# A fused decoder block on one core: another model of time for ordering each engine's instructions

## The chip, the cores and the metric

The kernel runs on one core of a Trainium2 chip. A core has five engines that run beside each other, each with its own queue of instructions that it takes in order: TensorE (matrix products, PE in the profile), VectorE (DVE), ScalarE (ACT), GpSimd (POOL) and SyncE (SP, which here only issues DMA transfers). They wait for each other by semaphores. The metric is the device time of the whole program in microseconds, and lower is better.

## The reference

One layer of a decoder block on x of 1024 rows and 1024 columns. A normalised input goes through one wide projection, whose columns feed two attention branches and their gates.

```python
h = rms_norm(x, norm_in[layer])
proj = h @ w_in[layer]
(dq, dk, dv, dgate, cq, ckv, kr, mgate, g_diff, g_mla) = jnp.split(proj, split_idx, axis=-1)
# differential branch: 4 heads, 2 score maps of 64 columns each, values of 128
dq, dk = apply_rope(dq, cos_d, sin_d), apply_rope(dk, cos_d, sin_d)
o_diff = causal_multimap_attention(dq, dk, dv, [1, -lam], 64 ** -0.5)
o_diff = rms_norm(o_diff, diff_subln[layer]) * (1.0 - lambda_init) * silu(dgate)
# latent branch: 4 heads, queries from rank 384, keys and values from rank 256, 64 rotary columns
q = rms_norm(cq, mla_q_norm) @ w_uq
kv = rms_norm(ckv, mla_kv_norm) @ w_ukv
o_mla = causal_multimap_attention([q_nope, rope(q_rope)], [k_nope, rope(kr)], v, [1], 192 ** -0.5)
o_mla = o_mla * silu(mgate)
merged = sigmoid(g_diff) * (o_diff @ w_proj_diff) + sigmoid(g_mla) * (o_mla @ w_proj_mla)
return rms_norm(x + merged @ w_out, norm_final)
```

## The kernel before

**Products.** A float32 product runs as three passes over operands that are split exactly into a high and a low part: high by high (line 160), then the two mixed ones (161, 162; `mm3`). `split` makes the parts: a cast on ScalarE (line 152) and a subtraction on VectorE or GpSimd (line 153).

**Stages.** First the values of the differential branch (`bank`, eight banks of PSUM, TensorE's result memory), then two sweeps for the latent columns `cq`, `ckv`, `kr`, whose weights are `wcr` (loaded), `wch`, `wcl` (split). Between these, ScalarE, VectorE and GpSimd split the values (`vst_h`, `vst_l`, three buffers each) for stores to DRAM (`d_dv`). `latent_turns` turns the latents by transposes (line 531) through `tp` and `pv`, and stores them (`d_c`, line 537); its last two blocks are the shared key, which `rotate` (lines 487 to 490: shuffle, product, product, sum) puts through the buffers `rt1` and `rt2`, two of each.

Then four heads of the differential branch. `project` makes 128 columns of queries, keys or gates in 48 products, in two banks named `mm`; `rotate` also reads the queries and keys from there. Scores (`sc`, two buffers, lines 628 and 629) go through a softmax (line 435 on VectorE, 438 on ScalarE) to the probabilities `e`. `values` multiplies them by the values for one group of 512 queries: for each block of 128 keys, four or fewer transposes (line 457) into `tp`, which has one buffer; from it the cast `ph` and the subtraction `pl`; then three products into `pv` (lines 160 to 162). The last block is one product (line 474). The second group has seven such steps before that one; their widths are five times 512 columns, then 384 and 256. `diff_norm` squares the result (642), splits the square in three (652 to 655) beside the product with the gate (656), sums it on TensorE (662) and scales the result (666 to 683).

After head 3, `latent_load` and `latent_begin` bring the latents back (`craw`), split them (`ch` on ScalarE, `cl` on VectorE or GpSimd) and start the latent branch, whose first weights are `wknh` and `wknl`. Merge, output product and final normalisation end the program.

**What sets the order.** The author emits the work in an order of his own: generators yield TensorE's time in each step, and `fill` puts steps of a queue (projections, mostly) between the steps of scores and values. The framework then sorts each engine's instructions once more, by their place in that order among those that are ready in a modelled time. Tiles, buffers and semaphores follow from the program and the pools.

Of the kernel before, what the change touches and what calls it, by code (L numbers as in the profile page):

```python
"""Hybrid decoder block: differential attention and multi-head latent attention on one
RMS-normalised input, merged by sigmoid gates, on one core.

Float32 products run as fp32r passes: every operand x is split exactly into hi = fp32r(x)
and lo = x - hi, and hi*hi + hi*lo + lo*hi is accumulated in float32.
"""
# [15 lines left out]
DRAM = bass.MemoryType.DRAM  # L22
# [29 lines left out]
def emit(tc, a):  # L52
    nc = tc.nc
    V, A, G, T = nc.vector, nc.scalar, nc.gpsimd, nc.tensor
# [21 lines left out]

    # ------------------------------------------------------------------ order of the work
    # Every engine runs its instructions in the order they are emitted. Work comes as
    # generators; each step yields the tensor engine's time in it (ns). A main stream yields
    # instead the time that its next step has to wait for, which is filled from `queue`.  # L80
    queue = deque()
# [40 lines left out]

    # ------------------------------------------------------------------ constants
    const = pool("const", "left")
# [44 lines left out]

    # DRAM scratch  # L170
    d_dv = [one(dram, [4, P, NB - 1, P], F32, f"d_dv{i}") for i in range(2)]
# [7 lines left out]

    # ------------------------------------------------------------------ normalised input, dv  # L180
    ht = pool("ht", "right")
# [8 lines left out]
    posi = one(p0, [P, S], I32, "posi")  # L190
    # keeps the tensor engine active until the first inputs are there
    cold = mk(p0, [P, 512], BF16, "cold", 1)
# [43 lines left out]

    # statistics of x
    ssq = one(p0, [P, NB], F32, "ssq")
# [6 lines left out]

    # lambda
    lam = one(p0, [P, 4, 64], F32, "lam")
# [27 lines left out]
    for b in range(NB):  # L275
        v = mk(p0, [P, 512], F32, "vst", 8)
# [14 lines left out]

    # projections of the input, 128 columns at a time; weights come one projection ahead
    plan = deque()
    ahead = deque()
# [24 lines left out]
    def rope_tables():  # L319
        """Two-stage reduction of the angles, then sine and cosine, a few steps at a time."""  # L320
        ang, r, kk, k2 = [mk(p0, [P, S], F32, "big", 6) for i in range(4)]
        V.tensor_copy(r, posi)
        yield
        V.tensor_scalar(ang, r, invf, None, op0=ALU.mult)
        yield
        V.tensor_scalar(kk, ang, 1.0 / (TWO_PI * COARSE), MAGIC, op0=ALU.mult, op1=ALU.add)
        yield
        V.tensor_scalar(kk, kk, MAGIC, None, op0=ALU.subtract)
        yield
        V.scalar_tensor_tensor(ang, kk, -COARSE * TP1, ang, op0=ALU.mult, op1=ALU.add)  # L330
        yield
        V.scalar_tensor_tensor(r, kk, -COARSE * (TWO_PI - TP1), ang, op0=ALU.mult, op1=ALU.add)
        yield
        V.tensor_scalar(k2, r, 1.0 / TWO_PI, MAGIC, op0=ALU.mult, op1=ALU.add)
        yield
        V.tensor_scalar(k2, k2, MAGIC, None, op0=ALU.subtract)
        yield
        V.scalar_tensor_tensor(r, k2, -TP1, ang, op0=ALU.mult, op1=ALU.add)
        yield
        for c in (TP2, TP3):  # L340
            V.scalar_tensor_tensor(r, kk, -COARSE * c, r, op0=ALU.mult, op1=ALU.add)
            V.scalar_tensor_tensor(r, k2, -c, r, op0=ALU.mult, op1=ALU.add)
        V.tensor_scalar(r, r, PI_IN, -PI_IN, op0=ALU.min, op1=ALU.max)
        yield
        A.activation(ang, r, AF.Abs)
        yield
        A.activation(cosp, ang, AF.Sin, scale=-1.0, bias=halfpi)
        yield
        A.activation(sinp, r, AF.Sin, scale=sgn)
        yield  # L350
        nc.sync.dma_start(d_rope[0], cosp)
        nc.sync.dma_start(d_rope[1], sinp)

    # ------------------------------------------------------------------ cq, then ckv and kr
    tables = rope_tables()
# [44 lines left out]

    # ------------------------------------------------------------------ shared work space
    wk = pool("wk", "left")
# [25 lines left out]
    def scores_tile(W):  # L428
        """Room for W columns, rounded up to what is computed, with no product across a bank's end."""
        sc = mk(ps, [P, S], F32, "sc", 2)  # L430
        return sc[:, P:S] if W == 640 else sc
# [14 lines left out]
    def values(g, probs, v_of, tp_of, gap):  # L446
        """o^T [dv, 512 queries of group g] = sum over key blocks of v^T p^T. The last block,
        of 128 queries, is one float32 product."""
        nk = 4 * g + 4
# [58 lines left out]

    # ------------------------------------------------------------------ differential branch
    rbc = one(p1, [P, S], F32, "rbc")  # L510
# [15 lines left out]
    def latent_turns():  # L526
        """The latents and the shared key, normalised, with the columns on the partitions."""
        for i, (c, n) in enumerate((c, n) for c in (0, 1, 2, 3, 4, 5) for n in range(2)):
            tp = mk(ps, [P, 512], F32, ("tp", "pv")[i % 2], 1)
            for j in range(4):  # L530
                T.transpose(tp[:, blk(j)], craw[c // 3][4 * n + j][:, blk(c % 3)], ident)
            if c < 5:
                t = mk(wk, [P, 512], F32, ("u", "g", "rt1", "rt2")[i % 4], 2)
                A.activation(t, tp, AF.Identity, scale=(g_q + g_kv)[c], bias=0.0)
            else:
                t = rotate(tp, cosp[:, half(n)], sinp[:, half(n)])
            nc.sync.dma_start(d_c[c][:, half(n)], t)
            yield 436
# [299 lines left out]

    # ------------------------------------------------------------------ latent branch
    ch, cl, cos, sin = latent["ch"], latent["cl"], latent["cos"], latent["sin"]  # L840
# [131 lines left out]
    drain()  # L972
    # ------------------------------------------------------------------ merge and output
    p3 = {}
# [56 lines left out]
    def group_and_next(h):  # L1031
        """Scores of a head's second group, with the next head's keys between them."""
        other = up_k(h + 1, latent_w[h + 1])
        for i, cost in enumerate(mla_group_scores(h, 1)):
            yield cost
            if i < 2:
                for _ in range(2):
                    yield next(other)
# [128 lines left out]

    # the last rows: the columns before the last quarter are weighted while that is computed
    b = NB - 1
# [43 lines left out]
def _layout(inp):  # L1213
    """The arrays as the kernel reads them: slices, permutations and transposes only."""
    x = np.asarray(inp["x"])[0]
# [54 lines left out]
```

## Time and profile before

| | before |
|---|---|
| runs, us | 904.51 median (901.31, 904.51, 906.76) |
| profiled execution, span | 901.6 us |
| TensorE busy | 873.8 us, 97% |
| VectorE, ScalarE, GpSimd busy | 557.1, 356.1, 245.3 us |
| moved by DMA | 96.70 MB |
| chain that ended last | TensorE 73%, VectorE 13%, DMA 6% |

The span runs from the profiled execution's first instruction to its last. Busy shares are means over the span. A wait is idle time of an engine put down to the instruction that ended it; the granted clock is a share of TensorE's full speed (2.4 GHz; the lower level is 1.2 GHz).

### The profile page before, as it was taken

What the parts mean: (1) busy time and instruction counts of PE and PEld (TensorE: products, weight loads), DVE (VectorE), ACT (ScalarE), POOL (GpSimd) and SP (SyncE); (2) the same over time, 40 slices, a digit from 0 to 9 for tenths busy, and PEclk for the clock granted to TensorE, in tenths of its full rate; (3) what the DMA queues carried; (4) which work ended last, traced back from release to release, by engine and by line L of the source; (5) the groups of instructions that cost most, each with busy time, mean ns of one, the idle gap of its engine ahead of it and who ended that gap; (6) DMA issues with size and microseconds to landing.
All of it is one profiled execution on the core that took longest, in us unless ns stands there. A gap on an engine that the chain in (4) does not pass through costs nothing.

```text
span 901.6 us, 11584 instructions
## 1 busy us (share of the span) xinstructions
PE 873.8 (97%) x4272; PEld 725.5 (80%) x4272; DVE 557.1 (62%) x1039; ACT 356.1 (39%) x686; POOL 245.3 (27%) x179
## 2 busy tenths in 40 slices
PE   9989999999998999989999999999999999999997
PEld 6779988888887888878878788778877778888886
DVE  5573247838278482884867766786677765561432
ACT  5752262434333343333434333645455532221211
POOL 2432013522234222342225231622313212210001
PEclk9999999999999999999999999999999999999999
DMA  7764035122221222222211215410104655434141
GB/s 283 296 194 157 23 120 184 54 84 73 81 71 61 91 71 83 70 64 89 71 59 32 86 38 184 158 36 24 48 24 152 199 171 185 147 95 150 58 176 47
DMA packets 48824, 96.70 MB, mean 107 GB/s; under 512 B 4992, under 2 KB 17536, under 8 KB 48768
## 3 DMA queue, kind: packets, MB, share of 16 engines
q1 hardware_dynamic: 46176, 89.81, 30.2%
q0 software_dynamic: 1152, 3.67, 1.3%
q10 hardware_dynamic: 1440, 2.49, 0.7%
q8 instruction: 33, 0.54, 0.2%
q14 instruction: 23, 0.19, 0.1%
HBM read 68.96 MB, written 27.00 MB: 106 GB/s over the span
## 4 chain that ended last, share of the span: by engine, by line
PE 73%; DVE 13%; DMA 6%; ACT 3%; issue 2%; POOL 2%; SPq 0%; POOLq 0%; DVEq 0%; ACTq 0%
PE mm L160 14%; PE mm L162 13%; PE mm L161 13%; PE acc L160 3%; PE acc L161 3%; PE acc L162 3%; PE tp L457 2%; PE sc L628 2%; PE bank L161 2%; PE bank L160 2%; DVE rt L489 2%; PE bank L162 2%; PE sc L629 2%; DVE kl L506 2%; PE pv L161 2%
## 5 line engine op out<-in xcount | busy, mean ns | idle before, releaser
L160 PE MATMUL mm<-hh,wh 128*128 128x512 f32 x512 | 203.4, 397 | 4.6 <-DVE g L579 4.6
L162 PE MATMUL mm<-hh,wl 128*128 128x512 f32 x512 | 201.2, 393 | 0.0
L161 PE MATMUL mm<-hl,wh 128*128 128x512 f32 x512 | 200.8, 392 | 0.0
L153 POOL TENSOR_TENSOR wl<-wr,wh 128x1024 fp32r<-128x1024 f32 x32 | 82.0, 2565 | 195.3 <-ACT wh L152 191.2
L160 PEld LDWEIGHTS mm<-hh,wh 128*128 128x128 f32 x512 | 96.8, 189 | 23.2 <-issue 4.9
L162 PEld LDWEIGHTS mm<-hh,wl 128*128 128x128 f32 x512 | 96.7, 189 | 21.0
L161 PEld LDWEIGHTS mm<-hl,wh 128*128 128x128 f32 x512 | 96.9, 189 | 18.4
L435 DVE CUSTOM_DVE_ANT_0 sc<-sc,mask 128x128 f32<-128x128 f32 (+7 forms) x96 | 71.6, 773 | 8.8 <-PE sc L912 8.7
L438 ACT ACTIVATE e<-sc,mn 128x128 f32<-128x128 f32 (+3 forms) x64 | 47.5, 743 | 67.4 <-DVE mn L435 64.6
L153 DVE TENSOR_TENSOR pl<-tp,ph 128x512 fp32r<-128x512 f32 (+2 forms) x52 | 31.5, 606 | 61.2 <-ACT ph L152 61.0
L152 ACT CAST ph<-tp 128x512 fp32r<-128x512 f32 (+2 forms) x52 | 27.0, 520 | 83.0 <-PE tp L457 82.4
L160 PE MATMUL acc<-woh,mh 128*128 128x512 f32 (+1 forms) x136 | 51.7, 380 | 0.0
L161 PE MATMUL acc<-wol,mh 128*128 128x512 f32 (+1 forms) x136 | 51.7, 380 | 0.0
L162 PE MATMUL acc<-woh,ml 128*128 128x512 f32 (+1 forms) x136 | 51.7, 380 | 0.0
L160 PE MATMUL bank<-wch,hh 128*128 128x384 f32 (+1 forms) x128 | 42.3, 331 | 3.5 <-ACT wch L152 3.5
L921 POOL TENSOR_TENSOR e<-e,rs 128x128 f32<-128x128 f32 (+5 forms) x24 | 24.9, 1042 | 73.1 <-DVE rs L443 73.0
L152 ACT CAST wh<-wr 128x1024 fp32r<-128x1024 f32 x32 | 33.6, 1049 | 27.1 <-PE mm L161 14.9
L161 PE MATMUL bank<-wcl,hh 128*128 128x384 f32 (+1 forms) x128 | 42.1, 329 | 0.6 <-DVE wcl L153 0.6
L162 PE MATMUL bank<-wch,hl 128*128 128x384 f32 (+1 forms) x128 | 41.9, 328 | 0.0
L153 POOL TENSOR_TENSOR wpl<-wpr,wph 128x512 fp32r<-128x512 f32 x16 | 22.0, 1376 | 70.2 <-ACT wph L152 61.1
L579 DVE TENSOR_TENSOR g<-mm,rbc 128x512 f32<-128x512 f32 x40 | 27.5, 687 | 20.3 <-PE mm L162 20.2
L582 ACT ACTIVATE u<-g 128x512 f32<-128x512 f32 x40 | 25.2, 630 | 29.7 <-DVE g L579 24.3
(291 smaller groups left out, 1943.9 us busy)
## 6 DMA issues: line engine op xcount, KB each, us to landing
wr<-in_w_t SPq DMA_DIRECT2D x32, 512.0 KB, 3.6
d_t<-u SPq DMA_DIRECT2D x32, 256.0 KB, 2.0
tg<-d_t SPq DMA_DIRECT2D x32, 256.0 KB, 2.8
big<-in_x SPq DMA_DIRECT2D x8, 512.0 KB, 7.6
wor<-in_w_out SPq DMA_DIRECT2D x8, 512.0 KB, 4.7
xres<-in_x SPq DMA_DIRECT2D x8, 512.0 KB, 4.9
big<-in_xT SPq DMA_DIRECT2D x7, 512.0 KB, 7.1
craw<-d_c SPq DMA_DIRECT2D x5, 512.0 KB, 6.7
```

Of the source, the lines that this page charges most:

```text
L152: A.copy(hi, src)
L153: (eng or V).tensor_tensor(lo, src, f32(hi), op=ALU.subtract)
L160: T.matmul(ps, lhsT=lh, rhs=rh, start=first, stop=False)
L161: T.matmul(ps, lhsT=lh, rhs=rl, start=False, stop=False)
L162: T.matmul(ps, lhsT=ll, rhs=rh, start=False, stop=last)
L435: V.tensor_tensor_reduce(sc[:, 0:W], sc[:, 0:W], mask[:, S - W:S], scale=-scale, scalar=BIG, op0=ALU.add, op1=ALU.min, accum_out=mn)
L438: A.activation(dst, sc[:, 0:W], AF.Exp, scale=-1.0, bias=mn, accum_out=sm)
L457: T.transpose(tp[:, blk(j)], probs[j][:, blk(kb)], ident)
L489: (eng or V).tensor_tensor(t2, t2, sin, op=ALU.mult)
L579: V.tensor_tensor(g, b, rbc[:, half(n)], op=ALU.mult)
L582: A.activation(u, g, AF.Tanh, scale=0.5 / by)
L921: G.tensor_tensor(e, e, r.broadcast_to([P, W]), op=ALU.mult)
```

## The change

The only line of the program that differs makes the context in which the kernel is emitted; with the new argument, the framework sorts each engine's instructions by another, finer model of the time that each takes. The other differences blank comments and docstrings.

```diff
-    with tile.TileContext(nc) as tc:
+    with tile.TileContext(nc, schedule_with_timeline_sim=True) as tc:
         emit(tc, a)
```

Each engine has the same instructions as before. Places change for 3090 of TensorE's 4362, 781 of VectorE's 1019, 347 of ScalarE's 562, 79 of GpSimd's 184 and 154 of SyncE's 280. Three places follow. In the rows, the number behind a name tells the buffer's use apart, and left of the arrow stands what is written.

TensorE where the last block of the shared key is turned (`pv_227`), before: the products next to it belong to a gate (`mm_212`); `mm_232`, `mm_241`, `mm_247` and `mm_250` are the projections that follow, and `mm_250` begins at row 765 in both orders.
```order
L531 MATMUL pv_227_1360<-ident_67,raw_185_1151 128x128
L531 MATMUL pv_227_1360<-ident_67,raw_187_1155 128x128
L160 MATMUL mm_212_1293<-hh6_93,wh_167_1118 128x512
L161 MATMUL mm_212_1293<-hl6_101,wh_167_1118 128x512
L162 MATMUL mm_212_1293<-hh6_93,wl_168_1119 128x512
```

TensorE at the same transposes, after: they stand between products of `mm_241`.
```order
L531 MATMUL pv_227_1360<-ident_67,raw_185_1151 128x128
L531 MATMUL pv_227_1360<-ident_67,raw_187_1155 128x128
L161 MATMUL mm_241_1435<-hl6_101,wh_170_1124 128x512
L162 MATMUL mm_241_1435<-hh6_93,wl_171_1125 128x512
L160 MATMUL mm_241_1435<-hh7_94,wh_170_1124 128x512
L161 MATMUL mm_241_1435<-hl7_102,wh_170_1124 128x512
L162 MATMUL mm_241_1435<-hh7_94,wl_171_1125 128x512
L160 MATMUL mm_247_1474<-hh0_87,wh_222_1343 128x512
```

The transposes moved from row 686 to 735; between them and row 765 stand 78 products before and 29 after.

TensorE in the second group of head 0's values (`pv_418`), before, from the products of one step to the next step's first transpose; `mm_417` is a projection.
```order
L161 MATMUL pv_418_2221<-pl_414_2203,dvh_256_1558 128x512
L162 MATMUL pv_418_2221<-ph_413_2202,dvl_257_1559 128x512
L160 MATMUL mm_417_2214<-hh2_89,wh_372_2019 128x512
L161 MATMUL mm_417_2214<-hl2_97,wh_372_2019 128x512
L162 MATMUL mm_417_2214<-hh2_89,wl_373_2020 128x512
L160 MATMUL mm_417_2214<-hh3_90,wh_372_2019 128x512
L161 MATMUL mm_417_2214<-hl3_98,wh_372_2019 128x512
L162 MATMUL mm_417_2214<-hh3_90,wl_373_2020 128x512
L160 MATMUL mm_417_2214<-hh4_91,wh_372_2019 128x512
L161 MATMUL mm_417_2214<-hl4_99,wh_372_2019 128x512
L162 MATMUL mm_417_2214<-hh4_91,wl_373_2020 128x512
L457 MATMUL tp_425_2247<-ident_67,e4_346_1920 128x128
```

After, a whole step there, from transposes to transposes:
```order
L457 MATMUL tp_425_2247<-ident_67,e4_346_1920 128x128
L457 MATMUL tp_425_2247<-ident_67,e5_361_1987 128x128
L457 MATMUL tp_425_2247<-ident_67,e6_380_2050 128x128
L457 MATMUL tp_425_2247<-ident_67,e7_393_2105 128x128
L161 MATMUL pv_418_2221<-pl_421_2228,dvh_256_1558 128x512
L162 MATMUL pv_418_2221<-ph_420_2227,dvl_257_1559 128x512
L160 MATMUL pv_418_2221<-ph_426_2252,dvh_256_1558 128x512
L457 MATMUL tp_430_2273<-ident_67,e4_346_1920 128x128
L457 MATMUL tp_430_2273<-ident_67,e5_361_1987 128x128
L457 MATMUL tp_430_2273<-ident_67,e6_380_2050 128x128
```

The nine products of `mm_417` between two steps are gone from here; they stand earlier. The second group of head 1 (`pv_645`) and of head 3 (`pv_1093`) read alike after.

TensorE at the end of head 3's first group, before, ahead of the first variance product; `sq0` and `sq1` are parts of the square of `pv_996`, `mm_1028` is a projection.
```order
L160 MATMUL mm_1028_4819<-hh3_90,wh_983_4626 128x512
L161 MATMUL mm_1028_4819<-hl3_98,wh_983_4626 128x512
L162 MATMUL mm_1028_4819<-hh3_90,wl_984_4627 128x512
L662 LDWEIGHTS sq0_1011_4771
L662 MATMUL tp_1029_4832<-meanw_68,sq0_1011_4771 128x2
L662 LDWEIGHTS sq1_1012_4772
L662 MATMUL tp_1029_4832<-meanw_68,sq1_1012_4772 128x2
```

After, where `mm_1113` is the latent branch's first product, with the weight `wknh`:
```order
L161 MATMUL mm_1092_5096<-hl7_102,wh_1044_4881 128x512
L162 MATMUL mm_1092_5096<-hh7_94,wl_1045_4882 128x512
L474 MATMUL pv_996_4701<-plast_1195,dvf_920_4375 128x128
L662 LDWEIGHTS sq0_1011_4771
L662 MATMUL tp_1029_4832<-meanw_68,sq0_1011_4771 128x2
L662 LDWEIGHTS sq1_1012_4772
L662 MATMUL tp_1029_4832<-meanw_68,sq1_1012_4772 128x2
L160 MATMUL mm_1113_5222<-ch3_5173,wknh_1079_5039 128x512
```

Before, eight score products and 24 products of `mm_1008` and `mm_1028` stand between line 474's product and the first of line 662; after, none.

VectorE at the same place, before:
```order
L579 TENSOR_TENSOR g_1007_4743<-mm_995_4691,rbc_1200 128x512
L652 CAST sq0_1011_4771<-rt1_1010_4769 128x512
L656 SCALAR_TENSOR_TENSOR o_1014_4774<-pv_996_4701,gsub_72,du_924_4423 128x512
L653 TENSOR_TENSOR rt1_1010_4769<-rt1_1010_4769,sq0_1011_4771 128x512
L435 ISA sc_1020_4784,mn_1021_4789<-sc_1020_4784,mask_1194 128x640
L435 ISA mn_1021_4789 128x1
L654 CAST sq1_1012_4772<-rt1_1010_4769 128x512
```

and after:
```order
L579 TENSOR_TENSOR g_1101_5147<-mm_1092_5096,rbc_1200 128x512
L153 TENSOR_TENSOR cl3_5178<-craw3_5033,ch3_5173 128x512
L153 TENSOR_TENSOR cl4_5179<-craw4_5035,ch4_5174 128x512
L153 TENSOR_TENSOR cl3_5178<-craw3_5033,ch3_5173 128x512
L153 TENSOR_TENSOR cl4_5179<-craw4_5035,ch4_5174 128x512
L652 CAST sq0_1011_4771<-rt1_1010_4769 128x512
L656 SCALAR_TENSOR_TENSOR o_1014_4774<-pv_996_4701,gsub_72,du_924_4423 128x512
L153 TENSOR_TENSOR cl0_5175<-craw0_5027,ch0_5170 128x512
L653 TENSOR_TENSOR rt1_1010_4769<-rt1_1010_4769,sq0_1011_4771 128x512
L153 TENSOR_TENSOR cl2_5177<-craw2_5031,ch2_5172 128x512
L153 TENSOR_TENSOR cl1_5176<-craw1_5029,ch1_5171 128x512
L654 CAST sq1_1012_4772<-rt1_1010_4769 128x512
```

Seven `cl` subtractions now stand ahead of and among lines 652 to 654.

## Rows read from the trace of the kernel before

**Rows 1.** The page: the span, and each engine's busy time, share and instructions.
```profile
span 901.6 us, 11584 instructions
...
PE 873.8 (97%) x4272; PEld 725.5 (80%) x4272; DVE 557.1 (62%) x1039; ACT 356.1 (39%) x686; POOL 245.3 (27%) x179
```

**Rows 2.** The page's chain that ended last: shares of the span by engine.
```profile
PE 73%; DVE 13%; DMA 6%; ACT 3%; issue 2%; POOL 2%; SPq 0%; POOLq 0%; DVEq 0%; ACTq 0%
```

**Rows 3.** TensorE's waits: product, line, releaser and its line; us in total, times, longest.
```profile
PE mm L160 <- DVE g L579: 4.6, 2, 2.3
PE bank L160 <- ACT wch L152: 3.5, 1, 3.5
```

**Rows 4.** Busy time of each engine by stretch; then granted clock, DMA share, GB/s.
```profile
core 0: us, PE busy (x) PEld busy (x) DVE busy (x) ACT busy (x) POOL busy (x), PEclk, DMA share, GB/s
...
60.00:67.50 7.50, 3.39 (x19) 2.82 (x17) 2.28 (x4) 6.22 (x8) 2.40 (x2) 0.97 0.96 283
67.50:71.00 3.50, 3.50 (x12) 3.50 (x13) 1.45 (x3) 0.69 (x2) 0.00 (x1) 0.58 0.96 288
...
248.00:270.00 22.00, 22.00 (x113) 18.14 (x112) 17.47 (x30) 8.14 (x13) 7.77 (x6) 1.00 0.24 73
...
281.50:285.50 4.00, 4.00 (x14) 3.26 (x13) 3.63 (x7) 2.42 (x7) 2.37 (x1) 0.57 0.13 45
...
462.00:470.00 8.00, 6.63 (x34) 5.19 (x34) 6.64 (x9) 2.23 (x4) 2.40 (x1) 1.00 0.08 13
490.00:500.00 10.00, 8.32 (x40) 6.65 (x39) 7.64 (x12) 4.75 (x10) 9.20 (x6) 1.00 0.01 2
...
568.00:604.00 36.00, 33.72 (x164) 25.63 (x164) 30.29 (x56) 22.64 (x48) 20.39 (x17) 1.00 0.32 107
```

**Rows 5.** The chain from 128 us on: start us, us, what (spacing of products).
```profile
128.47 0.44 PE tp L531 x4
128.90 0.23 PE mm L160
```

**Rows 6.** The same chain around the store of the shared key's last block.
```profile
135.88 0.72 DVE rt L487
...
137.77 2.62 DVE rt L489
...
141.61 8.48 DMA d_c<-rt
...
150.11 0.69 DVE rt L488
```

**Rows 7.** DMA issues of 130 to 152 us: xcount, KB each, median us to landing.
```profile
d_c<-rt SPq DMA_DIRECT2D x3, 256.0 KB, 2.1
...
dvf<-d_df SPq DMA_DIRECT2D x2, 128.0 KB, 8.6
```

**Rows 8.** Groups of 225 to 275 us, forms apart: busy us, mean ns | idle before.
```profile
L457 PE MATMUL tp<-ident,e 128*128 128x128 f32 x26 | 4.1, 272 | 0.0
...
L153 DVE TENSOR_TENSOR pl<-tp,ph 128x512 fp32r<-128x512 f32 x5 | 3.5, 692 | 11.9 <-ACT ph L152 11.9
...
L152 ACT CAST ph<-tp 128x512 fp32r<-128x512 f32 x5 | 2.9, 582 | 8.3 <-PE tp L457 8.3
...
L642 ACT ACTIVATE rt<-pv 128x512 f32<-128x512 f32 x1 | 0.6, 599 | 1.8 <-PE pv L474 1.8
```

**Rows 9.** The tile `cl`, its subtraction on VectorE: xcount: ns min/median/max, first and last start.
```profile
L153 DVE TENSOR_TENSOR cl<-craw,ch x7: 676/693/1264, 567.3 to 575.4; 128x512 fp32r<-128x512 f32 x7
```

**Rows 10.** VectorE's timeline in head 2's normalisation: start us, us, operation.
```profile
527.93 0.75 DVE L656 SCALAR_TENSOR_TENSOR o<-pv,gsub,du 128x512 f32<-128x512 f32 x1
528.59 0.68 DVE L653 TENSOR_TENSOR rt<-rt,sq 128x512 f32<-128x512 f32 x1
...
529.93 0.42 DVE L654 CAST sq<-rt 128x512 bf16<-128x512 f32 x1
...
531.01 0.69 DVE L655 TENSOR_TENSOR sq<-rt,sq 128x512 bf16<-128x512 f32 x1
```

## The prediction

> **What bounds the kernel now.** I read the page first. TensorE is busy 873.8 of 901.6 us, VectorE 62% of it, ScalarE 39% [rows 1], and 73% of the chain that ended last is TensorE [rows 2]. So the end is set by TensorE's matmuls plus what TensorE waits for, and since the change adds and removes no instruction, only the waits and the granted clock can move the time. The list of TensorE's waits comes next: the long ones of before are a few, each a place where a product stands right behind something VectorE or ScalarE must finish [rows 3]. The table of stretches then tells where TensorE has no slack and where it stands idle [rows 4]: from 248 to 270 it is busy for 22.00 of 22.00 us, in 60 to 67.5 for 3.39 of 7.50. The reader should see in it that before is nearly closed: about 28 us of idle in all.
>
> The profiled span of 901.6 us lies 2.9 us (0.3%) under the median of 904.51 us; the sum below is made on the span and its difference is put on the median.
>
> **The change, term by term.** The order decides which matmul stands behind which wait. A matmul of 512 columns takes TensorE 0.23 us, four transposes 0.44 us [rows 5].
>
> A, head 0's first projections (near 135 us in before). The last turned block of the shared key goes through shuffle, product, product, sum on VectorE and is stored; from the shuffle's start at 135.88 to the store's start at 141.61 are 5.7 us, the store takes 8.48, and only then may line 488 (0.69) of a later block overwrite the buffer (`rt1` has two) [rows 6]. That line frees the bank that a later product `mm_250` needs. Before, 78 matmuls (687 to 764) stand between the transposes and `mm_250`, 78 x 0.227 = 17.7 us: nothing is lost. After, 29 do (736 to 764), 6.6 us. The path is 5.7 + 0.6 (line 487 to 489 of another block now lie between, where two other operations lay) + 8.5 + 0.7 = 15.5, so TensorE waits 15.5 - 6.6 = 8.9 us. Bounds: stores of this kind land in 2.1 us where they are alone, in 8.6 the slowest load of that stretch [rows 7]: 2.5 to 9.0. I take 8.9, since the loads that delay it (`dv` of head 0) still stand near it, and SP now issues the store behind two of them (`dvf`) and not ahead.
>
> B, the second group's value loops of heads 0 and 1. Before, nine matmuls of a projection stand between two steps of such a loop. After, none do: a step is four transposes, the cast `ph`, the subtraction `pl`, and the next four transposes must wait for `pl`, because `tp` has one buffer. A step of 512 columns then lasts 0.16 + 0.44 (four transposes with the last one's 0.27 in place of 0.11) + 0.58 + 0.69 [rows 8] + 0.09 for four hops of 0.02 (the store of A ends at 150.09, line 488 starts at 150.11 [rows 6]) = 1.96 us, with 0.44 + 3 x 0.227 = 1.12 of work for TensorE in it: 0.84 lost. Three such steps lose 2.5; the three narrower ones (384, 256 and 128 columns), where each part shrinks, I estimate at 0.6, 0.5 and 0.35. So 3.9 per loop, 7.8 for two. Nothing covers it: TensorE takes its instructions in order, so whatever stands behind the waiting transposes (the scores of the next head, its projections) waits too, and VectorE and ScalarE find their later work late by as much. Bounds 6 to 9.
>
> C, from head 3 to the latent branch (near 565 us). Before, 32 matmuls stand between the last value product (`pv_996`) and the first variance product (line 662). After, none. What lies between is the square (0.60 [rows 8]) and the cast line 652 (as line 654, 0.42 [rows 10]), and VectorE has four `cl` subtractions in front of it (0.69 each, [rows 9]): 0.60 + 4 x 0.69 + 0.42 = 3.8 us. The second variance product waits for lines 656, 653, 654 (0.75 + 0.68 + 0.42 [rows 10]) and three more `cl`: 3.9 us. The first latent weight (`wknh`, `wknl`) now stands behind ten casts on ScalarE and three `cl` on GpSimd; for it I put one split, 0.58 + 0.69 [rows 8] = 1.3. Sum 9.0. Below: without any `cl` in the way 1.0 + 1.9 = 2.9; above: 12, where the loads that `ch` waits for come late, since the square stands behind four of those casts on ScalarE's queue.
>
> D, head 3's second loop is bare as well, with four full steps: 4 x 0.84 + 1.45 = 4.8. Behind it six matmuls (1.4 us) stand ahead of its variance, where square and cast take 1.0 and the four operations behind them 0.75 + 0.68 + 0.42 + 0.69 = 2.5 [rows 10] against nine matmuls (2.1); with what VectorE has beside it I put 2.2. Sum 7.0, bounds 5 to 9.
>
> E, waits of before that go. From 60 to 67.5 TensorE stands idle 4.1 us, because the first weights of the next sweep (`wch`, `wcl`) stand on ScalarE and VectorE behind splits that wait for a store to leave a buffer; the new order puts them ahead of those. The clock fell to 0.58 behind it [rows 4]: of 3.50 us at 0.58 the share of 0.42 is lost, 1.5 us. So -5.6, bounds -6 to 0 (nothing, if the store only holds up another step). The idle in 462 to 470 (1.4), 490 to 500 (1.7) and 568 to 604 (2.3) is gone too in the new order, where more matmuls stand ahead of those products: -5.4, bounds -6 to 0. Sum -11.0.
>
> F, near 281 and 394 (line 579, 4.6 us in two [rows 3]) the same products stay behind the same operations: 0. Behind 604 us the order differs by a few places: 0, bounds -3 to 3.
>
> G, the clock. Behind the wait near 281 (2.3 us in this list [rows 3]) the granted clock is 0.57 from 281.5 to 285.5 [rows 4], the 1.2 GHz level for most of it: 4.00 x 0.43 = 1.7 us lost. Behind the waits in 462 to 470 and 490 to 500 those stretches show 1.00. A and C bring two places with longer waits than the one near 281: +3.4, bounds 0 to 5.
>
> Sum: 8.9 + 7.8 + 9.0 + 7.0 - 11.0 + 3.4 = +25.1 us; 901.6 + 25.1 = 926.7 in the span, 904.5 + 25.1 = 929.6 against the median. I say 930.
>
> **A rule beside G.** In before, the two falls of the clock in these rows stand behind one long wait each, and the stretches with waits of 1.3 to 1.8 us stay at 1.00 [rows 4]. The Trainium skill, TensorE: Matmul & The Clock Gate, section HAM oscillation — how this bites in real kernels, says that regular gaps between bursts of matmuls can bring the clock down again and again, and not only one long wait. By that rule the bare loops of B and D would run at half clock in part. Whether the trace agrees is open: before has no such loop. What it would give is the second rival, whose time is worked out from rows.
>
> **Rivals.**
> Smaller loss. B and D's loop are fixed by the single `tp` buffer; A and C depend on when stores and loads land. With the store in 2.1 us (A 2.5), C at its lower end (2.9), D 5 and one clock drop (1.7): 2.5 + 7.8 + 2.9 + 5 + 1.7 - 11.0 = +8.9, 913. For it: three stores of that stretch have a median of 2.1 us. Against: the one that counts took 8.48.
> Larger loss. In the bare loops the clock also falls to 1.2 GHz: TensorE's 0.44 + 0.68 double where they stand on the step's path (the transposes, 0.44 more), so 1.96 becomes 2.4; with 19 steps in three loops 19 x 0.44 = 8.4, and C at 12: 25.1 + 8.4 + 3 = +36.5, 941. For it: each step has a wait. Against: each is short beside the waits behind which the clock fell.
> The other side. The terms that cost rest on a loop step being longer than its matmuls. If TensorE reaches the transposes of a step 1.96 us after those of the step before, because an earlier wait (A's or C's) has let ScalarE and VectorE run ahead, then nothing is lost; that holds for the first step only, as `tp` has one buffer, which is why I give it little. With A at 2.5, C at 2.9, B and D at half (7.4), no clock drop and E at -12: +0.8; faster by over 0.5% only if B and D are below 3 together. 900 to 905.
> That the order isn't changed can be put aside: 3090 of TensorE's instructions stand elsewhere.
>
> **Chances.** My forecast (+18 to +31) 0.64, smaller loss (+5 to +18) 0.17, larger (over +31) 0.12, no loss 0.07. Predicted 930 us. From 913 to 946 holds 8 in 10: 913 is the smaller loss as worked out, 946 the larger one with A's and G's upper bounds. A measurement tells 0.5% (4.5 us) from no change: faster 0.03, same 0.05, slower 0.92.
>
> **What would show it.** A: one wait of 8 to 9 us of TensorE with VectorE's line 488 as its releaser, and that held by a store; B and D: `tp` (line 457) waiting for `pl`, about 0.8 us each, some 10 full ones, step to step 1.96 us; C: two waits of nearly 4 us at line 662; E: no long wait for `wch`. Wrong would be: a store in A that lands in 2 us, loop steps under 1.5 us, or new waits in 604 to 890, where I put none.

## The result and the profile after

The changed kernel takes 932.03 us (median of 4 runs, 930.94 to 932.84) beside 904.98 us of the kernel before in the same series: 1.0303 times as long, with a 95% interval of 1.0278 to 1.0327. The forecast was 930 us.

The page of the profiled execution, its span and busy times, against [rows 1]:

```profile
span 929.7 us, 11587 instructions
...
PE 883.6 (95%) x4272; PEld 728.9 (78%) x4272; DVE 561.6 (60%) x1039; ACT 355.4 (38%) x686; POOL 243.9 (26%) x179
```

The span is 28.1 us longer, while TensorE's busy time grows by 9.8 only. So about 18 us are waits that the profile shows as idle; the rest counts as busy: work at the lower clock, and products with a gap behind them, which count longer (0.48 us in the bare loop below, 0.39 where the next product stands right behind). TensorE's waits show where (columns as in [rows 3]):

```profile
PE mm L160 <- DVE rt L488: 9.0, 5, 5.8
PE tp L662 <- DVE sq L654: 7.1, 1, 7.1
PE pv L160 <- ACT ph L152: 4.0, 13, 0.7
PE tp L662 <- DVE e L654: 3.8, 1, 3.8
PE tp L662 <- DVE sq L652: 3.3, 1, 3.3
PE tp L457 <- DVE pl L153: 3.0, 14, 0.3
PE mm L457 <- DVE part L1023: 1.9, 1, 1.9
...
PE mm L160 <- DVE g L579: 0.4, 2, 0.2
```

Of the two long entries of [rows 3], `wch` is gone and line 579 is down to 0.2 us each. In their place stand line 488 (term A), `ph` and `pl` in many short pieces (B and D) and line 662 (C and D). By stretch, with the columns of [rows 4] (us, busy time of each engine, granted clock, DMA share, GB/s):

```profile
60.00:67.50 7.50, 7.50 (x45) 7.50 (x44) 1.72 (x3) 1.75 (x4) 2.46 (x2) 1.00 0.99 311
147.00:153.20 6.20, 0.44 (x3) 0.04 (x1) 2.26 (x6) 0.01 (x1) 0.00 (x0) 0.69 0.92 317
153.20:158.00 4.80, 4.80 (x15) 3.87 (x16) 4.67 (x8) 2.89 (x5) 0.94 (x1) 0.68 0.02 7
249.00:267.00 18.00, 16.03 (x74) 10.92 (x73) 9.70 (x14) 4.51 (x8) 2.44 (x2) 1.00 0.10 30
...
462.00:500.00 38.00, 38.00 (x182) 31.55 (x181) 25.99 (x49) 12.79 (x24) 12.80 (x7) 1.00 0.17 57
565.00:576.50 11.50, 1.08 (x8) 0.72 (x6) 10.93 (x13) 8.56 (x18) 7.74 (x6) 0.68 0.69 254
576.50:582.00 5.50, 5.50 (x23) 3.81 (x22) 2.27 (x3) 0.59 (x1) 5.50 (x6) 0.50 0.29 97
592.00:606.00 14.00, 10.81 (x47) 6.07 (x48) 5.04 (x8) 4.12 (x9) 0.00 (x0) 1.00 0.05 16
606.00:612.00 6.00, 1.76 (x9) 1.21 (x8) 5.44 (x7) 3.73 (x7) 2.94 (x2) 0.85 0.26 86
612.00:620.00 8.00, 8.00 (x37) 6.18 (x37) 5.89 (x15) 2.31 (x7) 2.39 (x2) 0.69 0.09 26
...
732.00:770.00 38.00, 34.79 (x160) 28.06 (x161) 24.19 (x39) 16.90 (x29) 4.50 (x4) 0.96 0.56 180
```

The idle stretch at 60 us is closed, and so is 462 to 500. TensorE stands still for 5.8 of 6.2 us before 153.2, 10.4 of 11.5 before 576.5 and 4.2 of 6 before 612, and behind each of these the granted clock is near 0.5 to 0.7: the 1.2 GHz level for part of the stretch. In the bare loop of head 0, which runs from 257 to 267, the clock stays at 1.00 (row 249 to 267).

Term A in the chain of waits (start us, us, what):

```profile
145.14 7.25 DMA d_c<-rt
...
152.41 0.70 DVE rt L488
...
153.16 0.80 PE mm L160
153.96 0.43 PE mm L161
```

The store lies on TensorE's path for 7.25 us, line 488 follows, and then the first products come 0.43 us apart instead of 0.23.

A step of the bare loop on TensorE's timeline (start us, us, operation, in brackets the idle time before it and its releaser):

```profile
256.93 0.60 PE L457 MATMUL tp<-ident,e 128*128 128x128 f32 x4
...
258.25 0.50 PE L160 MATMUL pv<-ph,dvh 128*128 128x512 f32 x1 [0.27 <-ACT ph L152]
259.02 0.66 PE L457 MATMUL tp<-ident,e 128*128 128x128 f32 x4 [0.27 <-DVE pl L153]
```

From transposes to transposes are 2.09 us (forecast 1.96), with a short wait for `ph` and one for `pl`; the next two full steps take 2.06 us each. The loop of term D, in head 3, runs from the first of these lines to the second, 14.3 us, with five full steps of 2.00 to 2.11 us and the three narrower ones:

```profile
591.34 0.60 PE L457 MATMUL tp<-ident,e 128*128 128x128 f32 x4
...
605.62 0.48 PE L160 MATMUL mm<-wvh,ch 128*128 128x512 f32 x1
```

Term C in the chain, ahead of the second wait: lines 653 and 654 with `cl` subtractions between them.

```profile
569.54 1.11 DVE cl L153
570.65 1.67 DVE rt L653
572.33 3.08 DVE cl L153 x2
575.40 0.88 DVE sq L654
```

The subtractions take 1.1 to 1.5 us there, not the 0.69 of [rows 9], and line 653 takes 1.67 us, not 0.68 [rows 10]. The four `cl` subtractions ahead of them on VectorE's timeline, and GpSimd's own, which begin when those four are done:

```profile
566.15 2.49 DVE L153 TENSOR_TENSOR cl<-craw,ch 128x512 fp32r<-128x512 f32 x4
```

```profile
568.76 4.70 POOL L153 TENSOR_TENSOR cl<-craw,ch 128x512 fp32r<-128x512 f32 x3 [11.82 <-DMA sinm<-d_rope]
```

So VectorE's operations take 0.62 us each before GpSimd begins, and up to about two and a half times their time beside it.

The start, by the products of the first latent sweep, whose last column says when the first and the last of them began; the kernel before, then the changed one:

```profile
L160 PE MATMUL bank<-wch,hh x128: 307/340/522, 50.1 to 117.8; 128*128 128x384 f32 x64, 128*128 128x320 f32 x64
```

```profile
L160 PE MATMUL bank<-wch,hh x128: 307/324/341, 49.1 to 110.6; 128*128 128x384 f32 x64, 128*128 128x320 f32 x64
```

The last product comes 7.2 us earlier, of which 1.0 was there at the first: more than the 5.6 forecast for the start. So the changed kernel loses 35 us after 111 us to end 28 behind.

### The profile page after: what moved, and what is told of

Same layout as the page of the kernel before. It is cut to its first block, busy times and chain, and to the rows that moved or that the text cites. A ratio compares the mean times of both kernels' runs of the same rounds, so it can differ in the third digit from the quotient of the medians.

```text
span 929.7 us, 11587 instructions
## 1 busy us (share of the span) xinstructions
PE 883.6 (95%) x4272; PEld 728.9 (78%) x4272; DVE 561.6 (60%) x1039; ACT 355.4 (38%) x686; POOL 243.9 (26%) x179
## 3 DMA queue, kind: packets, MB, share of 16 engines
q1 hardware_dynamic: 46176, 89.81, 28.5%
## 4 chain that ended last, share of the span: by engine, by line
PE 80%; DVE 10%; DMA 4%; ACT 2%; issue 2%; POOL 0%; SPq 0%; POOLq 0%; DVEq 0%; ACTq 0%
PE mm L160 15%; PE mm L162 15%; PE mm L161 15%; PE bank L160 4%; PE bank L162 4%; PE bank L161 4%; PE acc L160 3%; PE acc L162 3%; PE acc L161 3%; PE tp L457 2%; PE sc L629 2%; PE sc L628 2%; DVE kl L506 1%; DVE pl L153 1%; DMA omr<-d_om 1%
## 5 line engine op out<-in xcount | busy, mean ns | idle before, releaser
L435 DVE CUSTOM_DVE_ANT_0 sc<-sc,mask 128x128 f32<-128x128 f32 (+7 forms) x96 | 72.2, 768 | 28.5 <-PE sc L629 20.9
L160 PE MATMUL bank<-wch,hh 128*128 128x384 f32 (+1 forms) x128 | 39.6, 324 | 0.0
```

Source lines behind the costliest of these rows:

```text
L160: T.matmul(ps, lhsT=lh, rhs=rh, start=first, stop=False)
L435: V.tensor_tensor_reduce(sc[:, 0:W], sc[:, 0:W], mask[:, S - W:S], scale=-scale, scalar=BIG, op0=ALU.add, op1=ALU.min, accum_out=mn)
```

## The experiments

"By hand" means that instructions of the named engines keep the order in which the author's code emits them, in the named part of the program; the other engines and parts are left to the finer model. The edits are one context around the part:

```diff
+    with tc.manual_schedule(engines={mybir.EngineType.PE}):
         ...
```

Times are medians; the ratio is to the kernel before in the same series. The kernel before has 903 to 905 us in the four series, so a difference to the changed kernel can be read from the times or from the ratios, and the two readings differ by 1 to 2 us.

**1. TensorE by hand everywhere** (the context above around the whole of `emit`).

> The changed kernel, but TensorE issues in the author's order from end to end; the other four engines are still sorted by the finer model. Theory (the loss is TensorE's order alone): the waits near 141 to 153, 569 to 576 and 611 us and the bare value loops go, and the shorter start stays, since it comes from ScalarE's and VectorE's order: 905 - 7 = 898 us, between 893 and 906. Rival (the order of VectorE, ScalarE, GpSimd and SyncE costs as much, above all the cl subtractions ahead of the normalisation): at least half of the loss stays, 917 us or more.

Measured: 912.96 us, 1.0108 (1.0089 to 1.0127). Between theory and rival: 18 (by the ratios) or 19 (by the times) of the 27 us are TensorE's order, and the waits named in the expectation are gone, but a new one of 8.9 us stands at 568 us, where a transpose waits for `pl`. VectorE and GpSimd at that time:

```profile
559.17 8.77 DVE L153 TENSOR_TENSOR cl<-craw,ch 128x512 fp32r<-128x512 f32 x6
567.87 0.68 DVE L153 TENSOR_TENSOR pl<-tp,ph 128x512 fp32r<-128x512 f32 x1
```

```profile
559.62 4.71 POOL L153 TENSOR_TENSOR cl<-craw,ch 128x512 fp32r<-128x512 f32 x3 [14.01 <-ACT ch L152]
```

Six `cl` subtractions stand in VectorE's queue ahead of `pl` and take 8.77 us, in which GpSimd works nearly throughout (after its three `cl`, on weights until 567.4 us).

**2. TensorE by hand in the turning of the latents and head 0's first projections.**

> The changed kernel, but TensorE issues in the author's order from the turning of the latents to the end of head 0's first projections. Theory (term A): the two waits for line 488 (1.6 and 5.8 us) and the half clock behind the second (1.5 us in 153 to 158) go, as 78 instead of 29 products cover the store: 932 - 9 = 923 us, 921 to 925. Rival (the store is slow because it lies beside the loads of dv, and something waits for it in any order): 929 us or more, with the wait at another product.

Measured: 922.07 us, 1.0215 (1.0198 to 1.0233). That is 10.0 us less than the changed kernel by the times and 8.0 by the ratios. The theory holds: both waits and the fall of the clock are gone, and the last value product of head 0 begins at 258.4 instead of 266.9 us, 8.5 us earlier. The rest of the time is not A's alone. C's first wait grew from 3.3 to 5.5 us:

```profile
PE tp L662 <- DVE sq L652: 5.5, 1, 5.5
```

Against that, the wait at line 1023 in the latent branch is 1.5 us here instead of 1.9, with no fall of the clock behind it.

**3. TensorE by hand in heads 0 and 1.**

> The changed kernel, but TensorE issues in the author's order within heads 0 and 1, so that products of the projections stand between the steps of the value loops again. Theory as predicted (term B, with term F at nothing): two loops lose 5.3 us each in the changed kernel and 1.0 in the kernel before, so 932 - 8.6 = 923 us. Rival (F was wrong: the waits of the kernel before near 281 and 394, 2.4 us and a half clock each, come back, because they are the price of filling the loops): 932 - 8.6 + 6.5 = 930 us.

Measured: 922.63 us, 1.0219 (1.0201 to 1.0238). The theory holds: 9.4 us less by the times, 7.6 by the ratios, and the last value product of head 2 begins at 508.6 instead of 516.3 us, 7.7 us earlier. Behind it C's first wait grew to 5.5 us here too. The waits for line 579 come back at 1.0 us each, not at 2.3, and without a fall of the clock; so most of what was gained there comes from the order of the other engines and is not a price of the loops.

**4, 5, 6. Head 3 by hand: TensorE alone; all engines; all but TensorE.**

> The changed kernel, but TensorE issues in the author's order within head 3, up to the first products of the latent branch. Theory (terms C and D with their half clock): the waits at line 662 (3.3, 7.1 and 3.8 us) are covered again, the loop at 592 us is filled, and the clock stays up in 576 to 582 and 612 to 620: 932 - 19 = 913 us, 909 to 918. Rival (the normalisation waits for VectorE's cl subtractions and those for loads from DRAM, so that TensorE's order only moves the wait): 925 us or more.

> The changed kernel, but all engines issue in the author's order within head 3 (before, only TensorE did, and VectorE's queue then held the loop's subtraction pl behind six cl subtractions). Theory (C and D are VectorE's queue and TensorE's lack of cover together): no wait above 2 us between 500 and 640, and no half clock there: 932 - 19 = 913 us, 909 to 917. Rival (the loads of the latents come late, whatever the order): 925 us or more.

> The changed kernel, but VectorE, ScalarE and GpSimd issue in the author's order within head 3; TensorE keeps the finer model's order, with nothing between the last value product and line 662. Theory (most of C is VectorE's queue): the two waits at line 662 (3.3 and 7.1 us) shrink to what square, cast and lines 656, 653, 654 need, 1.1 and 1.9, and the half clock behind them goes (2.7 us): 932 - 10 = 922 us; the loop and the later variance stay. Rival (it is TensorE's order alone): 930 us or more.

Measured: 936.33 us, 1.0370 (1.0354 to 1.0385); 940.08, 1.0405 (1.0386 to 1.0423); 941.60, 1.0428 (1.0408 to 1.0448). All three are slower than the changed kernel. The rivals' bounds (925, 925 and 930 us or more) are met, but not for their reasons, and none foresaw a time above 932. These edits undo more than C. In experiment 4, TensorE's timeline has waits where there were none, at head 2's last normalisation:

```profile
506.98 0.18 PE L662 MATMUL tp<-meanw,sq 128*128 128x2 bf16 x1 [1.15 <-DVE sq L652]
510.85 0.19 PE L662 MATMUL tp<-meanw,sq 128*128 128x2 bf16 x1 [3.69 <-DVE sq L654]
513.96 0.43 PE L662 MATMUL tp<-meanw,sq 128*128 128x2 bf16 x10 [2.92 <-DVE sq L655]
517.12 0.80 PE L681 MATMUL tp<-rt1r,onesr 128*128 128x512 f32 x1 [2.74 <-POOL rt1r L675]
```

These are 10.5 us, where the changed kernel has 0.4 us of idle from 500 to 565 us. The finer model had covered them with products of head 3, which the author's order holds back. Experiment 5 has the same four waits, experiment 6 the last two (2.6 and 2.7 us). Behind them, in experiment 4, the 8.9 us wait for `pl` of experiment 1 appears again. So the three say that the order of one head can't be put back alone; on C and D they say nothing.

**7. Experiment 1 without `cl` on GpSimd.**

```diff
-                split_latent(c, n, (None, G)[(c + n) % 2])
+                split_latent(c, n)
```

> The first experiment's kernel (TensorE by hand, 913 us), but GpSimd's three cl subtractions are done on VectorE. There, six of VectorE's stood ahead of pl and took 8.77 us, up to 1.75 each, while GpSimd ran its own; now eight stand ahead of pl. Theory (they are slow because GpSimd works at the same time): about 0.61 apart, 4.9 us, so the wait of 8.9 us falls to 5 and the time to 909. Rival (they are slow by themselves or wait for the casts): eight at 1.46, 11.7 us, a wait of some 12 us and 916.

Measured: 906.80 us, 1.0039 (1.0025 to 1.0052). VectorE's timeline:

```profile
557.48 4.89 DVE L153 TENSOR_TENSOR cl<-craw,ch 128x512 fp32r<-128x512 f32 x8
```

Eight take 4.89 us, 0.61 apart, where six took 8.77, and the wait for `pl` is 5.1 us instead of 8.9. For the subtractions the theory holds to the tenth: VectorE's were slow because GpSimd worked beside them; here GpSimd begins only in the last us of the eight. The time fell by 6.2 us, of which this wait is 3.9; 1.7 more lie ahead of the first latent sweep, which this edit doesn't touch (its first product begins at 49.6 instead of 51.3 us). The Trainium skill, GPSIMD Engine Reference, section 1. Specifications, says that GpSimd shares its interfaces to on-chip memory with VectorE, and that operations of VectorE with two inputs from there contend; these traces agree, 0.61 against up to 1.75 us for the same subtraction.

**8. TensorE by hand everywhere, all engines by hand in head 3.**

> The first experiment's kernel (TensorE by hand, 913 us), with all engines by hand within head 3. Theory: its wait of 8.9 us for pl and the half clock behind it go, and nothing takes their place: 913 - 11 = 902 us, and if the shorter start (7 us) is worth what the trace shows, 897. Rival (the wait only moves to the next instruction that needs the latents): 909 or more.

Measured: 911.37 us, 1.0095 (1.0072 to 1.0118). The rival holds: the 8.9 us wait is gone, but five waits of 1.5 to 1.8 us stand between 552 and 593 us, and the last product with `wvh` behind them begins at 599.5 us, in experiment 1 at 601.1. By that much the first latent sweep is ahead already (its first product begins at 49.6 against 51.3 us), so nothing is gained here.

**9. The kernel before with the first latent splits ahead.**

```diff
-        split(wh[:, 0:width], wl[:, 0:width], wr[:, 0:width])
+        with tc.high_priority(offset=40):
+            split(wh[:, 0:width], wl[:, 0:width], wr[:, 0:width])
```

> The kernel before, with one thing of the new order alone: the splits of the first latent weights (wch, wcl) stand ahead of the last splits of the values, on ScalarE (one moved) and VectorE (seven moved). Theory (term E's first half, which the changed kernel gains and loses again elsewhere): 4.1 us of idle and 1.5 us of half clock near 60 to 71 go, and everything behind comes earlier by as much: 904 - 5.6 = 898 us, 896 to 900. Rival (a later wait, for instance for a load, takes it back): 902 or more.

Measured: 901.95 us, 0.9985 (0.9973 to 0.9996). Some of the wait stays:

```profile
60.00:67.50 7.50, 5.49 (x25) 4.92 (x24) 4.42 (x7) 5.60 (x8) 1.27 (x1) 0.86 0.97 285
67.50:71.00 3.50, 3.50 (x18) 3.50 (x17) 0.00 (x0) 0.00 (x0) 1.65 (x1) 0.80 0.94 259
```

TensorE stands idle 2.0 us instead of 4.1, and the clock still falls somewhat. The changed kernel's full gain at the start (7.2 us) therefore needs more than these splits (here the last product of the sweep comes 2.8 us earlier); it also issues the weights' loads and the other splits in another order, which wasn't tried apart. The time is the rival's, but no later wait takes the gain back: the profiled span is 2.4 us shorter. The gain itself is half of what the theory put. No kernel of the series is clearly faster than the kernel before; this one comes nearest, and its 0.15% is less than the 0.5% that was set as the bound of what can be told.

**10. The changed kernel with `cl` behind line 655.**

`latent['norm']` is line 655's instruction in head 3's first normalisation; `issue_after` puts instructions of the block behind it in its engine's order.

```diff
...
+        with tc.issue_after(latent['norm']):
             split(latent["ch"][c][:, half(n)], latent["cl"][c][:, half(n)], latent["raw"][c][:, half(n)], eng)
```

> The changed kernel; only VectorE's cl subtractions are put behind line 655 of head 3's first normalisation (seven rows of VectorE and one of ScalarE move, none of TensorE). Theory (C is VectorE's queue): the waits of 3.3 and 7.1 us at line 662 shrink to 2.4 and 1.9, and the half clock behind them (2.7 us) goes: 932 - 8 = 924 us. Rival (the latents have to be split before TensorE can go on in any case, so the wait moves to the first latent products, which need cl): 930 to 932 us, with a wait of TensorE for cl at line 161.

Measured: 929.98 us, 1.0296 (1.0277 to 1.0315). The rival holds. TensorE's waits (line 664 is what line 662 was):

```profile
567.40 0.18 PE L664 MATMUL tp<-meanw,sq 128*128 128x2 bf16 x1 [1.15 <-DVE sq L652]
570.07 0.19 PE L664 MATMUL tp<-meanw,sq 128*128 128x2 bf16 x1 [2.50 <-DVE sq L654]
571.74 0.42 PE L664 MATMUL tp<-meanw,sq 128*128 128x2 bf16 x10 [1.49 <-DVE sq L655]
...
573.43 0.79 PE L161 MATMUL mm<-cl,wknh 128*128 128x512 f32 x1 [0.63 <-DVE cl L153]
...
575.97 0.79 PE L161 MATMUL mm<-cl,wknh 128*128 128x512 f32 x1 [1.32 <-DVE cl L153]
...
582.55 0.50 PE L160 MATMUL mm<-ch,wqnh 128*128 128x512 f32 x1 [2.37 <-DVE knl L153]
```

Together 9.5 us instead of 10.4: 5.1 at the variance, and new ones of 4.3 for `cl` and for `knl` behind it. The time is 2.0 us lower, and the intervals of the two ratios lie almost wholly over each other.

**11. The changed kernel with the loads of `dv` issued later.**

`latent_kl[0]` is GpSimd's last `kl` subtraction.

```diff
...
+        with tc.issue_after(latent_kl[0]):
             nc.gpsimd.dma_start(vh, d_dv[0][h])
             nc.gpsimd.dma_start(vl, d_dv[1][h])
```

> The changed kernel; only the loads of dv that GpSimd issues for heads 0 and 1 stand behind its kl subtractions, some 10 us later, away from the store of the shared key's last block (five rows of TensorE move). Theory (A's 7.3 us store is held up by these loads): the store lands in 2 to 3.5 us, the wait of 5.8 us falls below 2.5 and the half clock behind it goes: 932 - 5 = 927 us, 925 to 928. Rival (the store is as slow without them, because of SyncE's own load of weights beside it): 931 us or more.

Measured: 927.94 us, 1.0270 (1.0253 to 1.0287). The theory holds: 4.1 us less by the times, 3.0 by the ratios. The chain keeps the store ahead of the one in question, which took 3.48 us in the changed kernel, and the DMA issues of 136 to 154 us have both stores:

```profile
137.75 3.64 DMA d_c<-rt
```

```profile
d_c<-rt SPq DMA_DIRECT2D x2, 256.0 KB, 2.9
```

With a median of 2.9 us and one store of 3.64, the other one, which took 7.25 us, now takes about 2.2. It is off the chain, and its wait of 5.8 us with it. SyncE's own load of weights still stands right behind it, so the rival falls. The wait of 1.8 us ahead of it stays, and the clock now falls behind that one (0.66 in 142 to 147). C's first wait is 5.4 us here too.

**12. TensorE by hand in the turning of the latents and in heads 0, 1 and 2.**

> The changed kernel, with TensorE in the author's order in the turning of the latents and in heads 0, 1 and 2; head 3 and all behind it are left to the finer model, which there puts scores and projections between the last value product and line 662 again. Theory (A, B and C are all lack of cover on TensorE, and C comes of the state in which head 2 leaves the engines): A 10 and B 9.4 as measured apart, and C with its half clock some 8 to 10: 932 - 28 = 904 us, 900 to 908. Rival (C stays, since VectorE's queue is what holds it): 912 us or more.

Measured: 904.13 us, 1.0012 (0.9999 to 1.0026). The theory's number holds: by its time the changed kernel is back at the kernel before, with head 3 and all behind it still in the finer model's order. TensorE's longest waits there (the second is head 3's second group, D):

```profile
PE tp L457 <- DVE pl L153: 4.2, 4, 2.4
PE tp L662 <- DVE e L654: 3.9, 1, 3.9
```

The two waits at line 662 for the first normalisation of head 3 are gone, though head 3 itself was left to the finer model. Its order there has changed on both engines: from the last value product (530.0 us) to the first variance product (536.5) TensorE has other products to do, and VectorE's `cl` begin at 553.8 us, behind line 655 at 535.2. A part of C comes back at 553 to 560 us, as waits of 0.8 us for `cl` and 2.4 for `pl` behind it.

## Why the prediction was right, point by point

The time was right (930 and 932.03), and so was what sets its sign: products that had covered waits of TensorE stand elsewhere. A and B came by the mechanism that was forecast and within a fifth of their size. D was twice its forecast, C's size has a cause that its working lacked, and F, put at nothing, was wrong. These errors cancel, so that the hit within 2 us is in part luck.

Idle time alone makes a bare loop look cheaper than it is. So the terms are worked out here from the starts of TensorE's products in the two traces: how much later each next product begins than at full clock with nothing to wait for (0.227 us after one of 512 columns, 0.11 after a transpose), summed over the stretch and set against the kernel before. The half clock of G is in them; its forecast is put to A and C, 1.7 each.

| | forecast, us | from the traces, us |
|---|---|---|
| A | 10.6 | 9.4 |
| B, two loops | 7.8 | 9.3 |
| C | 10.7 | 14.1 |
| D | 7.0 | 14.2 |
| E, the start | -5.6 | -7.2 |
| E, the later waits | -5.4 | -8.5 |
| F | 0 | -5.5 |
| behind 604 us | 0 | 3.5 |
| the rest | | -0.8 |
| sum | 25.1 | 28.5 |

The span grew by 28.1 us; the counting is good to about half a us.

A: waits of 1.6 and 5.8 us and a fall of the clock came in place of one wait of 8.9 and a fall. Experiment 11 shows that the store's length beside the `dv` loads was the point on which it hung, as the text had it.

B: 4.7 us per loop instead of 3.9. The full step was 2.06 to 2.09 us instead of 1.96, and the narrower ones lost more than the estimate.

C: the waits were forecast at 3.8, 3.9 and 1.3 us; they were 3.3, 7.1 and none. The first is as worked out. In the second, lines 653 and 654 and the `cl` subtractions took up to about two and a half times their time, because GpSimd runs its own beside them (experiment 7). The fall of the clock cost more too, 2.8 us instead of 1.7. Taking `cl` out of VectorE's way gives nothing (experiment 10), since the products that need the latents then wait. What makes C, as far as is shown, is that no products are left between the last value product and line 662: the order of the heads before decides that, for with heads 0 to 2 by hand the model itself covers it (experiment 12). There VectorE's `cl` moved away as well; cover alone was not tried, as experiments 4 to 6 undid too much, and neither was the changed kernel without `cl` on GpSimd.

D: this is the term that was mis-sized. Its loop lost 7.0 us, not 4.8: five full steps stand in it, not four. The wait for the variance, with the one behind it, was 4.2 us, not 2.2: VectorE's lines 490 and 653 took 1.36 and 1.75 us there, while GpSimd subtracted `krl`. And a third fall of the clock, 2.5 us, came behind it, where G counted two. No experiment shows D apart.

E: more idle went than forecast. The later waits can't be told cleanly from C and D, which now stand in the place of 568 to 604.

F: this step failed, and its reason with it, that the same products stay behind the same operations. The waits for line 579 shrank from 2.3 to 0.2 us each, beside which 0.5 for line 488 stands now, and the falls of the clock behind them went. Experiment 3 points to the order of the other engines, since most of the gain stays with the loops filled.

G, forecast +3.4 for two falls: there are three, 4.80 x 0.32 = 1.5, 5.50 x 0.50 = 2.8 and 8.00 x 0.31 = 2.5, together 6.8.

Behind 604 us a wait of 1.9 us at line 1023 and a clock of 0.96 over 38 us (1.5) are new; the prediction had named new waits there as a sign of being wrong. Its range up to 946 doesn't come out of its own terms: the larger loss of 941 with A's and G's upper bounds (0.1 and 1.6 us more) is 943.

The rival of a larger loss, by which the clock would fall in the bare loops (which the prediction draws from the Trainium skill, TensorE: Matmul & The Clock Gate, section HAM oscillation — how this bites in real kernels, whose own case is a loop that waits for DMA in each round), didn't come: 249 to 267 shows 1.00, with TensorE waiting a few tenths of a us twice in each step, and so does 592 to 606. Here the measurement decides. The rival of no loss fell with the time itself, and that of a smaller one with the 7.25 us store and the 7.1 us wait of C.

## What to carry to other kernels

When only an order changes, count what stands between a producer's last instruction and its consumer on the busiest engine, and set that cover against the whole path through other engines and stores; that gave A and B within a fifth. Price the operations of that path with what the other engines do at that moment: C and D came out too small because VectorE's were priced as they run with GpSimd idle. Terms that are put at nothing need the same count, as F shows. A part of an order can't be judged by putting that part alone back: what it had lent to its neighbours comes back as waits there.

## What the runs showed of the hardware that was not expected

A subtraction of 128 x 512 on VectorE with both inputs in on-chip memory took 0.62 us in a row of four while GpSimd stood idle (changed kernel) and 0.61 in a row of eight, beside GpSimd only in its last us (experiment 7); it took 8.77 / 6 = 1.46 us, up to 1.75, while GpSimd subtracted too (experiment 1).

A 256 KB store took 7.25 us beside four loads of 448 KB of another queue, and about 2.2 us when these came later (experiment 11).

Loops in which TensorE waited 0.2 to 0.3 us twice in each step of 2.06 to 2.11 us kept a granted clock of 1.00 over 10 to 14 us.
